# The last projection of a decoder trunk: weight sums by adding transfers, and a plain tile between two formed products

## The chip, the cores and the metric

The kernel runs on one core of one Trainium2 chip. The core has TensorE (PE, matrix products into PSUM), VectorE (DVE), ScalarE (ACT), GpSimd (POOL) and SyncE (SP, which issues most transfers between HBM and SBUF). Each engine works off its own queue in order, and engines wait for each other by semaphores. The metric is the device time of one execution in microseconds; the time given for a kernel is the median of its runs.

## The reference

One residual layer on 512 positions of width 1024, in float32:

```python
u = rmsnorm(x, ln1_g)
proj = u @ w_in                       # split into q, k, v, pool, z, xbc, dt, gates
y_a = dilated_attention(q, k, v) @ w_a
y_b = pool_mixer(pool_in) @ w_b
y_c = ssd_mixer(z, xbc, dt) @ w_c
x = x + (gates[0]*y_a + gates[1]*y_b + gates[2]*y_c) @ w_o
h = causal_dwconv(rmsnorm(x, ln2_g) @ w_up)      # 512 x 5632
a, v = h[..., :2816], h[..., 2816:]
x = x + (silu(a) * v) @ w_down                   # 2816 x 1024
return rmsnorm(x, final_g)
```

The change concerns only the last two lines: the product with `w_down` (here "the last projection") and its surroundings.

## The kernel before

**Products in three parts.** TensorE gets each float32 operand as a high part (rounded to the type fp32r) and a low part (what is left). `mm3` (L228) runs high x high for all k, then high x low, then low x high, and sums them in PSUM. So every weight tile goes through the same steps: `fetch` (SP loads it, tile `raw`, two buffers), `cast` (ACT writes the high part `wh`, three buffers), `low` (DVE writes the low part `wl`, two buffers), then the products. A `Job` is one weight tile with its products. While job n runs on TensorE, `prepare` (L1605) issues the low part of job n+1, the cast of job n+2 and the load of job n+3; the cast is put off to the next `step()` inside the job, in two halves. A job may bring a `form` (what the cast takes as its source) and a `then` (called right after its low part is issued). The order of PE, ACT, DVE and POOL is the order in which the program issues; only SP's loads are placed by a scheduler.

**The up projection.** `up_jobs` has 22 jobs of 48 products each. They alternate between the two halves a and v, two column tiles at a time. `up_evac` (L1182) does the convolution on ACT (L1184) and DVE (L1187); in v's half POOL multiplies a and v (L1192), and the high and low parts of the result (`fh`, `fl`, L1199 and L1200) or sums of neighbours for the scheme below (`sums_of`) follow.

**The last projection.** Of the 22 tiles of 128 rows of `w_down`, the first 16 go as two groups of 8. Each group is a two by two block product in 7 products of quarters rather than 8 (Strassen's scheme in Winograd's form). Four of the seven weight operands are sums or differences of quarters. The jobs are called "one" to "seven"; each has 24 products (two position blocks x 12). Their jobs stand between the up jobs: `EARLY` places the first group after up jobs 8 to 14, `LATE` places four jobs of the second group after up jobs 18 to 21. The other six row tiles are plain: `blocks_of(0)` makes the left half of the columns in a job of 48 products and one of 24, `blocks_of(1)` the right half, with the norm and the output. `down` (L1300) gives the end of the kernel: "seven", first plain tile, "four", second plain tile, "three", right half.

**The weight sums.** `quarters(g)` gives the quarters q(two, h) in HBM. `load` puts q(0,1) and q(1,1) into two tiles W (tag `xs`). DVE forms each operand with `diff` (L339), a subtraction over 128x2048, in W or in a freshly loaded `raw`: after the low part of "one", and as the `form` of "six", "seven" and "four" (of the first group after "three"). That is four per group.

**Banks.** "one", "six", "seven" and "four" go on in the same two PSUM banks (X, names p1, p6, p7, p4; the profile prints them as `p`): each adds its product on what is there. After each of them `plus` (L1217) lets DVE add the bank to the sum X1, and the next may not write before that. "two", "five" and "three" share the banks Z.

**Norm.** When the left half of a position block is complete, `early` issues `norm_early`: a square sum on ACT (L438) and a product with the norm's weight on POOL (L462). `blocks_of(0)` asks for it for all four blocks.

The kernel is built with `dynamic_dma_scratch_size=1024`. Before the change no transfer is issued from POOL.

Of the kernel before, what the change touches and what calls it, by code (L numbers as in the profile page):

```python
# [13 lines left out]
OP = mybir.AluOpType  # L14
# [69 lines left out]
def trunk(ctx: ExitStack, tc, out, x, rel_bias, ln1_g, w_in, b_gate, w_a, pool_w, pool_scale, w_b,  # L84
# [235 lines left out]
    def sums_of(f0, f1, ah, al, found):  # L320
# [3 lines left out]
        dve.tensor_tensor(sa[:, LO], f0[:, HI], f1[:, HI], OP.add)  # L324
        dve.tensor_tensor(sa[:, HI], sa[:, LO], f0[:, LO], OP.subtract)
        dve.tensor_tensor(sb[:, LO], f0[:, LO], f0[:, HI], OP.subtract)
        dve.tensor_tensor(sb[:, HI], f1[:, LO], sa[:, HI], OP.subtract)
# [854 lines left out]
    def up_evac(m, ps):  # L1182
# [11 lines left out]
        def later():  # L1194
            yield
            k = m - KF
            if k >= KS or k % 2:
# [4 lines left out]
                if k < KS:  # L1202
                    yield
                    for _ in sums_of(HC[k - 1], a, T("sah", F32R), T("sal", F32R),
                                     lambda j, h, l: FS.__setitem__((j, k // 2), (h, l))):
                        yield
# [10 lines left out]
    def plus(tb, h, what):  # L1217
        dve.tensor_tensor(X1[tb, h], X1[tb, h], what, OP.add)
# [45 lines left out]
    def into(banks, name, adds, first=False, close=True):  # L1264
        def use(i, product):
# [3 lines left out]
            for tb, h in adds(i):  # L1269
                plus(tb, h, banks[i])  # L1270
        return use

    def sevens_down(g, keep=False):
# [4 lines left out]
        def load():  # L1278
            for h in range(2):
                W.append(ypool.tile([P, 4, S], F32, name="w3", tag="xs"))  # L1280
                sp.dma_start(W[h], q(h, 1))

        two = job(q(1, 0), side("A12"), into(Z, "p2", lambda i: [(i, 0)], True))
        one = job(q(0, 0), side("A11"), into(X, "p1", lambda i: [(i, 0)], True))
        one.then = lambda: diff(W[0], W[0], one.raw)
        five = job(None, side(1), into(Z, "p5", lambda i: [(2 + i, 1)], True), lambda: W[0])
        if keep:
            three = job(q(1, 1), side(4), into(Z, "p3", lambda i: [], close=False))
            six = job(None, side(2), into(X, "p6", lambda i: [(i, 1)]), lambda: diff(W[1], W[1], W[0]))
        else:  # L1290
            three = job(None, side(4), into(Z, "p3", lambda i: [(i, 1)]), lambda: W[1])
            three.then = lambda: diff(W[1], W[1], W[0])
            six = job(None, side(2), into(X, "p6", lambda i: [(i, 1)]), lambda: W[1])
        seven = job(q(0, 0), side(3), into(X, "p7", lambda i: [(2 + i, 1)]),
                    lambda: diff(seven.raw, W[1], seven.raw))
        four = job(q(1, 0), side("A22"), into(X, "p4", lambda i: [(2 + i, 0)]),
                   lambda: diff(four.raw, four.raw, W[1]))
        return load, dict(two=two, one=one, five=five, three=three, six=six, seven=seven, four=four), Z

    def down(rest, opened):  # L1300

        plain = blocks_of(0, {}, (), ())
        yield rest["seven"]
        yield next(plain)
        yield rest["four"]
        yield from plain
# [60 lines left out]
    def blocks_of(h, acc, opened, keep):  # L1367
        def evac(tb, ps):
            t = X1[tb, h]
            dve.tensor_tensor(t, t, ps, OP.add)  # L1370
            if h == 0:
                running.append(early(tb))
                return
# [291 lines left out]
```

## Time and profile before

| | before |
|---|---|
| median of 3 runs | 1039.03 us (1038.7 to 1039.3) |
| the profiled execution | 1038.0 us |
| its span, first to last instruction | 1036.2 us |
| mean granted TensorE clock | 0.998 |
| TensorE busy | 1024.7 us (99% of the span) |
| DVE, ACT, POOL busy | 676.2, 473.8, 149.6 us |
| moved by transfers | 120.76 MB |

The profile is of one execution; all its times count from the start of the span. A row of a timeline gives start, length, engine, line of the kernel, operation and `output<-input` with shapes, and in brackets how long the engine stood idle before it and what ended that. A row of a table of stretches gives for each engine its busy time and number of instructions, then the granted clock, the share of time that the 16 DMA engines were busy, and GB/s. In a row of groups `x2 | 4.6, 2288` means two instructions, 4.6 us together, 2288 ns each on average, and then the idle time before them. Matmuls overlap, so the length of one (about 0.39 us) is longer than its share of a row of them.

### The profile page before, as it was taken

How to read it: one execution, taken by the hardware profiler on the slowest of the kernel's cores; microseconds unless marked ns; L12 is line 12 of the kernel's file. 1: busy time of each engine (PE TensorE's matmuls, PEld its weight loads, DVE VectorE, ACT ScalarE, POOL GpSimd, SP SyncE). 2: the span in 40 equal slices, each digit the busy share in tenths (PEclk: the TensorE clock that was granted, in tenths of full speed). 3: DMA queues.
4: the chain of work that ended last, by engine and by line, in shares of the span. 5: the costliest groups of instructions: out<-in, count | busy, mean ns of one | idle time of the engine just before them, and what ended most of it. 6: DMA issues, size and time to landing. Idle time of an engine off the chain costs nothing.

```text
span 1036.2 us, 13090 instructions
## 1 busy us (share of the span) xinstructions
PE 1024.7 (99%) x5204; PEld 859.7 (83%) x5204; DVE 676.2 (65%) x907; ACT 473.8 (46%) x765; POOL 149.6 (14%) x125
## 2 busy tenths in 40 slices
PE   9999999999999999999999999999999999999997
PEld 9898878898888878888888888898888888888785
DVE  6553566684356658766768656766768677666855
ACT  6432544442564364557445324545444443443332
POOL 1770000000000004210152500001111001111110
PEclk9999999999999999999999999999999999999999
DMA  8344312126222344542244525543233224323232
GB/s 280 123 131 134 116 47 75 31 64 200 82 82 82 98 132 115 144 136 69 66 149 153 172 82 204 175 140 114 82 115 122 89 82 163 122 90 114 82 122 82
DMA packets 119069, 120.76 MB, mean 117 GB/s; under 512 B 5316, under 2 KB 101383, under 8 KB 119008
## 3 DMA queue, kind: packets, MB, share of 16 engines
q1 hardware_dynamic: 118415, 119.07, 36.4%
q8 instruction: 41, 0.67, 0.3%
q10 hardware_dynamic: 592, 0.86, 0.2%
q14 instruction: 21, 0.16, 0.1%
HBM read 116.12 MB, written 2.22 MB: 114 GB/s over the span
## 4 chain that ended last, share of the span: by engine, by line
PE 96%; DVE 1%; ACT 1%; DMA 1%; issue 0%; ACTq 0%; DVEq 0%
PE pa L234 35%; PE pu L234 22%; PE pb L234 11%; PE pqk L234 9%; PE p L234 8%; PE pa L1516 2%; PE ps L670 1%; PE pu L1324 1%; PE ppw L234 1%; PE pt L698 1%; PE po L711 1%; PE py L996 1%; DMA xin<-in_x_dram 1%; PE pyo L1003 1%; PE pst L982 0%; PE pxs L950 0%
## 5 line engine op out<-in xcount | busy, mean ns | idle before, releaser
L215 DVE TENSOR_TENSOR wl<-raw,wh 128x2048 fp32r<-128x2048 f32 (+3 forms) x95 | 218.8, 2305 | 50.2 <-ACT wh L195 40.6
L195 ACT CAST wh<-raw 128x1024 fp32r<-128x1024 f32 (+3 forms) x188 | 189.4, 1026 | 68.0 <-DVE raw L339 26.0
L1187 DVE SCALAR_TENSOR_TENSOR hc<-pu,fcol,hc 128x510 f32<-128x510 f32 x88 | 65.8, 747 | 58.9 <-ACT hc L1184 57.3
L234 PE MATMUL pa<-uh,wh 128*128 128x512 f32 x384 | 98.5, 398 | 0.0
L234 PE MATMUL pa<-ul,wh 128*128 128x512 f32 x384 | 94.9, 389 | 0.0
L234 PE MATMUL pa<-uh,wl 128*128 128x512 f32 x384 | 94.9, 389 | 0.0
L234 PEld LDWEIGHTS pa<-ul,wh 128*128 128x128 f32 x384 | 72.1, 188 | 15.2
L234 PEld LDWEIGHTS pa<-uh,wl 128*128 128x128 f32 x384 | 72.1, 188 | 15.0
L234 PE MATMUL pu<-uh,wl 128*128 128x512 f32 (+1 forms) x352 | 83.7, 380 | 0.0
L234 PE MATMUL pu<-uh,wh 128*128 128x512 f32 (+1 forms) x352 | 83.5, 379 | 0.0
L234 PE MATMUL pu<-ul,wh 128*128 128x512 f32 (+1 forms) x352 | 83.5, 379 | 0.0
L234 PEld LDWEIGHTS pa<-uh,wh 128*128 128x128 f32 x384 | 70.3, 188 | 14.7 <-issue 0.7
L234 PEld LDWEIGHTS pu<-uh,wl 128*128 128x128 f32 x352 | 64.1, 188 | 12.8 <-DVE wl L215 0.3
L234 PEld LDWEIGHTS pu<-ul,wh 128*128 128x128 f32 x352 | 64.2, 188 | 12.5
L234 PEld LDWEIGHTS pu<-uh,wh 128*128 128x128 f32 x352 | 64.1, 188 | 12.4
L1192 POOL TENSOR_TENSOR hc<-hc 128x512 f32<-128x512 f32 x22 | 30.5, 1388 | 278.9 <-DVE hc L1187 243.1
L1184 ACT ACTIVATE hc<-pu,fcol,fcol 128x512 f32<-128x512 f32 x40 | 31.2, 780 | 81.3 <-PE pu L234 81.0
L958 POOL TENSOR_TENSOR xd<-xc,dec 128x512 f32<-128x512 f32 x6 | 6.4, 1060 | 334.1 <-DVE xc L952 315.2
L1085 ACT ACTIVATE sg<-pa,col 128x512 f32<-128x512 f32 x24 | 16.5, 688 | 55.3 <-PE pa L234 48.6
L691 ACT ACTIVATE sb<-sb,both 128x128 f32<-128x128 f32 (+1 forms) x72 | 30.1, 419 | 23.5 <-DVE both L688 13.4
L234 PE MATMUL pqk<-uh,wh 128*128 128x512 f32 x144 | 36.9, 394 | 0.0
L234 PE MATMUL pqk<-ul,wh 128*128 128x512 f32 x144 | 36.3, 390 | 0.0
(352 smaller groups left out, 1793.2 us busy)
## 6 DMA issues: line engine op xcount, KB each, us to landing
raw<-in_w_in_dram SPq DMA_DIRECT2D x25, 1024.0 KB
raw<-in_ffn_w_up_dram SPq DMA_DIRECT2D x22, 1024.0 KB
raw<-in_ffn_w_down_dram SPq DMA_DIRECT2D x11, 1024.0 KB
raw<-in_w_in_dram SPq DMA_DIRECT2D x20, 512.0 KB
raw<-in_w_o_dram SPq DMA_DIRECT2D x8, 1024.0 KB
raw<-in_w_b_dram SPq DMA_DIRECT2D x4, 1024.0 KB
al<-ad SPq DMA_DIRECT2D x16, 256.0 KB
w<-in_ffn_w_down_dram SPq DMA_DIRECT2D x4, 1024.0 KB
```

The source lines that it names most:

```text
L195: act.copy(job.high[:, :, o], job.raw[:, :, o])
L215: (eng or dve).tensor_tensor(l[:, :, o], job.raw[:, :, o], h[:, :, o].bitcast(F32), OP.subtract)
L234: pe.matmul(ps, l, r, start=first and n == 0, stop=last and n == total - 1, skip_group_check=again)
L670: pe.matmul(pss[i][:, o:o + w * P], q[r, n * P:(n + 1) * P], k[r, kb * P:(kb + w) * P], start=True, stop=True)
L691: act.activation(sb[:, off:off + w * P], sb[:, off:off + w * P], AF.Exp, bias=nm[:, n, h:h + 1], accum_out=ls[:, n, h:h + 1])
L698: pe.transpose(pt[:, o:o + P], sb[:, o:o + P], eye)
L711: pe.matmul(po[DH * hh:DH * hh + DH, n * P:(n + 1) * P], V[g, kb + i][:, (2 * cc + hh) * DH:(2 * cc + hh + 1) * DH], probs[2 * cc + hh, mb ...
L1085: act.activation(s, ps, AF.Sigmoid, bias=col[:, o:o + 1])
L1184: act.activation(t, ps, AF.Identity, bias=ff["c1"][:, ff["b"] + m:ff["b"] + m + 1], scale=fw(2, m))
L1187: dve.scalar_tensor_tensor(t[:, sh:], ps[:, :S - sh], fw(k, m), t[:, sh:], OP.mult, OP.add)
L1192: pool.tensor_tensor(a, a, t, OP.mult)
L1516: pe.matmul(first[2 * n + j][:, lo:hi], a[:, k, j * P:(j + 1) * P], b[:, k, lo:hi], start=a is wh and b is uh and k == 0, stop=a is wl and ...
```

## The change

- The quarters are combined by adding only. `load` brings q(0,0) and q(0,1) into the two tiles W. After the low part of "one" is issued, POOL issues transfers from HBM that add q(0,1) to W[0] and q(1,1) to W[1]; after "five" they add q(1,1) to W[0], after "six" q(1,0) to W[0]. Each 1 MB is cut into two transfers of 512 KB. That is 8 transfers per group. The eight `diff` calls of the two groups go, and "one", "five", "six", "seven" and "four" take W as it is.
- The signs that this moves go to the other side: `sums_of` gets a sign for two of its four operations, and `plus` subtracts for "six" and "seven".
- "one" now comes before "two" in both groups, "three" always loads its quarter, and the second group's `load` is called two up jobs earlier.
- `down` is now: first plain tile, "seven", second plain tile, "four", "three", right half. `early` for position blocks 2 and 3 is issued after "four" instead of after the second plain tile.

```diff
--- before.py
+++ after.py
@@ -317,14 +317,14 @@
 
     LO, HI = slice(0, 256), slice(256, S)
 
-    def sums_of(f0, f1, ah, al, found):
+    def sums_of(f0, f1, ah, al, found, s=1):
 
 
         sa, sb = T("sa"), T("sb")
-        dve.tensor_tensor(sa[:, LO], f0[:, HI], f1[:, HI], OP.add)
+        dve.tensor_tensor(sa[:, LO], f0[:, HI], f1[:, HI], OP.add if s > 0 else OP.subtract)
         dve.tensor_tensor(sa[:, HI], sa[:, LO], f0[:, LO], OP.subtract)
         dve.tensor_tensor(sb[:, LO], f0[:, LO], f0[:, HI], OP.subtract)
-        dve.tensor_tensor(sb[:, HI], f1[:, LO], sa[:, HI], OP.subtract)
+        dve.tensor_tensor(sb[:, HI], f1[:, LO], sa[:, HI], OP.subtract if s > 0 else OP.add)
         yield
         bh, bl = T("sbh", F32R), T("sbl", F32R)
         act.copy(ah, sa)
@@ -1202,7 +1202,7 @@
                 if k < KS:
                     yield
                     for _ in sums_of(HC[k - 1], a, T("sah", F32R), T("sal", F32R),
-                                     lambda j, h, l: FS.__setitem__((j, k // 2), (h, l))):
+                                     lambda j, h, l: FS.__setitem__((j, k // 2), (h, l)), -1):
                         yield
                 return
             t = T("f0", F32R)
@@ -1214,8 +1214,8 @@
 
     FS = {}
 
-    def plus(tb, h, what):
-        dve.tensor_tensor(X1[tb, h], X1[tb, h], what, OP.add)
+    def plus(tb, h, what, op=OP.add):
+        dve.tensor_tensor(X1[tb, h], X1[tb, h], what, op)
 
     def first_half(p, i):
         return [t[:, i * P:(i + 1) * P] for t in FS[0, p]]
@@ -1261,13 +1261,15 @@
             return lambda p, i: second_half(p, i + 2 * (j == "A22"))
         return lambda p, i: sums(j, p, i)
 
-    def into(banks, name, adds, first=False, close=True):
+    def into(banks, name, adds, first=False, close=True, final=False):
         def use(i, product):
             if first:
                 banks[i] = SM(name)
             product(banks[i], first, close, not first)
-            for tb, h in adds(i):
-                plus(tb, h, banks[i])
+            for tb, h, *op in adds(i):
+                plus(tb, h, banks[i], *op)
+            if final:
+                running.append(early(2 + i))
         return use
 
     def sevens_down(g, keep=False):
@@ -1278,32 +1280,34 @@
         def load():
             for h in range(2):
                 W.append(ypool.tile([P, 4, S], F32, name="w3", tag="xs"))
-                sp.dma_start(W[h], q(h, 1))
+                sp.dma_start(W[h], q(0, h))
+
+        def adding(at, *what):
+            def then():
+                for w, part in zip(at, what):
+                    for k in (0, 2):
+                        pool.dma_start(W[w][:, k:k + 2, :], part[:, k:k + 2, :], accum_op=OP.add)
+            return then
 
         two = job(q(1, 0), side("A12"), into(Z, "p2", lambda i: [(i, 0)], True))
-        one = job(q(0, 0), side("A11"), into(X, "p1", lambda i: [(i, 0)], True))
-        one.then = lambda: diff(W[0], W[0], one.raw)
+        one = job(None, side("A11"), into(X, "p1", lambda i: [(i, 0)], True), lambda: W[0])
+        one.then = adding((0, 1), q(0, 1), q(1, 1))
         five = job(None, side(1), into(Z, "p5", lambda i: [(2 + i, 1)], True), lambda: W[0])
-        if keep:
-            three = job(q(1, 1), side(4), into(Z, "p3", lambda i: [], close=False))
-            six = job(None, side(2), into(X, "p6", lambda i: [(i, 1)]), lambda: diff(W[1], W[1], W[0]))
-        else:
-            three = job(None, side(4), into(Z, "p3", lambda i: [(i, 1)]), lambda: W[1])
-            three.then = lambda: diff(W[1], W[1], W[0])
-            six = job(None, side(2), into(X, "p6", lambda i: [(i, 1)]), lambda: W[1])
-        seven = job(q(0, 0), side(3), into(X, "p7", lambda i: [(2 + i, 1)]),
-                    lambda: diff(seven.raw, W[1], seven.raw))
-        four = job(q(1, 0), side("A22"), into(X, "p4", lambda i: [(2 + i, 0)]),
-                   lambda: diff(four.raw, four.raw, W[1]))
+        five.then = adding((0,), q(1, 1))
+        three = job(q(1, 1), side(4), into(Z, "p3", lambda i: [] if keep else [(i, 1)], close=not keep))
+        six = job(None, side(2), into(X, "p6", lambda i: [(i, 1, OP.subtract)]), lambda: W[0])
+        six.then = adding((0,), q(1, 0))
+        seven = job(None, side(3), into(X, "p7", lambda i: [(2 + i, 1, OP.subtract)]), lambda: W[1])
+        four = job(None, side("A22"), into(X, "p4", lambda i: [(2 + i, 0)], final=keep), lambda: W[0])
         return load, dict(two=two, one=one, five=five, three=three, six=six, seven=seven, four=four), Z
 
     def down(rest, opened):
 
         plain = blocks_of(0, {}, (), ())
+        yield next(plain)
         yield rest["seven"]
-        yield next(plain)
+        yield from plain
         yield rest["four"]
-        yield from plain
         yield rest["three"]
         yield from blocks_of(1, opened, (0, 1), ())
 
@@ -1369,7 +1373,8 @@
             t = X1[tb, h]
             dve.tensor_tensor(t, t, ps, OP.add)
             if h == 0:
-                running.append(early(tb))
+                if tb < 2:
+                    running.append(early(tb))
                 return
             v0, xg0 = fin[tb]
             for _ in norm_late(t, fin["g"], v0, lambda xg1: ((xg1, xg1), (xg0, xg0)),
@@ -1432,13 +1437,13 @@
         first, between, _ = sevens_down(0)
         second_, last_, opened = sevens_down(1, keep=True)
         extra = {EARLY + i: between[w] for i, w in enumerate(
-            ("two", "one", "five", "three", "six", "seven", "four"))}
-        extra.update({LATE + i: last_[w] for i, w in enumerate(("two", "one", "five", "six"))})
+            ("one", "two", "five", "three", "six", "seven", "four"))}
+        extra.update({LATE + i: last_[w] for i, w in enumerate(("one", "two", "five", "six"))})
         for i, job in enumerate(up_jobs()):
             yield job
             if i == EARLY - 3:
                 yield Call(first)
-            if i == LATE - 1:
+            if i == LATE - 3:
                 yield Call(second_)
             if i in extra:
                 yield extra[i]
```

## The prediction

> **What bounds the kernel now.** I read the head of the page first, then the stretches of the last projection one by one, then the order of time around the one hole that they show.
>
> ```profile
> span 1036.2 us, 13090 instructions
> PE 1024.7 (99%) x5204; PEld 859.7 (83%) x5204; DVE 676.2 (65%) x907; ACT 473.8 (46%) x765; POOL 149.6 (14%) x125
> PE 96%; DVE 1%; ACT 1%; DMA 1%; issue 0%; ACTq 0%; DVEq 0%
> ```
>
> TensorE is busy for 1024.7 of 1036.2 us and carries 96% of the chain that ended last. The change leaves the number of products as it is, so it can win only what lies in TensorE's holes, in the part of the span that it touches. The next fence is the table by stretches, from the first undisturbed product of the up projection to the end.
>
> ```profile
> core 0: us, PE busy (x) PEld busy (x) DVE busy (x) ACT busy (x) POOL busy (x), PEclk, DMA share, GB/s
> 689.12:972.90 283.78, 283.78 (x1298) 236.70 (x1297) 202.06 (x213) 123.66 (x163) 27.51 (x20) 1.00 0.32 105
> 923.90:945.70 21.80, 21.80 (x98) 18.06 (x97) 16.05 (x14) 10.59 (x14) 2.90 (x2) 1.00 0.35 117
> 945.70:962.00 16.30, 16.30 (x73) 13.49 (x73) 9.19 (x10) 5.00 (x7) 0.00 (x0) 1.00 0.20 65
> 972.90:980.04 7.14, 5.42 (x25) 4.17 (x24) 6.48 (x7) 4.86 (x6) 3.02 (x2) 1.00 0.00 0
> 980.04:1029.30 49.26, 49.24 (x216) 40.43 (x216) 30.28 (x45) 14.82 (x28) 7.10 (x4) 1.00 0.31 108
> 1029.30:1036.20 6.90, 0.00 (x0) 0.00 (x0) 2.72 (x8) 1.65 (x4) 0.00 (x0) 0.72 0.39 150
> ```
>
> From 689.12 to 972.90 TensorE has no hole, though VectorE makes seven of the eight sums there and is 71% busy. The only holes are 7.14 - 5.42 = 1.72 us before 980.04, and the 6.90 us after the last product. The granted clock is 1.00 up to the last product, so no clock is to be won.
>
> Now the hole itself, in order of time: "six" of the second group ends, "seven" (tiles p and sbh) starts.
>
> ```profile
> 973.31 1.30 POOL L1192 TENSOR_TENSOR hc<-hc 128x512 f32<-128x512 f32 x1 [28.92 <-DVE hc L1187]
> 974.65 0.62 ACT L1199 CAST fh<-hc 128x512 fp32r<-128x512 f32 x1
> 975.30 0.69 DVE L1200 TENSOR_TENSOR fl<-hc,fh 128x512 fp32r<-128x512 f32 x1
> 975.44 1.71 POOL L1192 TENSOR_TENSOR hc<-hc 128x512 f32<-128x512 f32 x1 [0.82 <-ACT fh L1199]
> 975.91 3.38 DVE L215 TENSOR_TENSOR wl<-raw,wh 128x2048 fp32r<-128x2048 f32 x1
> 979.22 0.67 DVE L1218 TENSOR_TENSOR x<-x,p 128x512 f32<-128x512 f32 x1
> 980.04 1.17 PE L234 MATMUL p<-wh,sbh 128*128 128x512 f32 x4 [1.72 <-DVE x L1218]
> ```
>
> "Seven" goes on in the banks that "six" filled, so it may not start before VectorE has added them to X1 (L1218). That add stands on VectorE behind the low part of the next weight tile, which runs until 979.29; TensorE waits 1.72 us.
>
> **The change part by part.** *The eight sums go from VectorE.*
>
> ```profile
> L339 DVE TENSOR_TENSOR w<-w,w 128x2048 f32<-128x2048 f32 x2 | 4.6, 2288 | 0.0
> L339 DVE TENSOR_TENSOR raw<-raw,w 128x2048 f32<-128x2048 f32 x2 | 4.6, 2287 | 1.2 <-DMA raw<-in_ffn_w_down_dram 1.2
> L339 DVE TENSOR_TENSOR raw<-w,raw 128x2048 f32<-128x2048 f32 x2 | 4.6, 2284 | 0.0
> L339 DVE TENSOR_TENSOR w<-w,raw 128x2048 f32<-128x2048 f32 x2 | 4.6, 2282 | 0.0
> ```
>
> 8 x 2.29 = 18.3 us of VectorE. Products hide all of it but the hole, so by itself it is worth 0. The changed signs (add for subtract) leave each instruction at its size: 0.
>
> *A plain tile between "six" and "seven", and another between "seven" and "four".* While the first plain tile runs, the two adds of "six" get done. Lengths, from the chain of waits:
>
> ```profile
> 945.68 10.88 PE pu L234 x48
> 956.56 5.44 PE p L234 x24
> 962.00 10.89 PE pu L234 x48
> ```
>
> One product takes 10.88/48 = 0.227 us. "Six" ends at 972.89 + 5.44 = 978.33, and the plain tile (48 products, 10.88 us) holds until 989.21; the adds of "six" end by about 981. "Seven" then finds its banks free, and likewise "four" behind 5.44 us of the second plain tile. Gain: 1.72 us. What is late next is the low part of that plain tile. It takes the place of the 3.38 us row above, which ends at 979.29; the plain tile needs it from its ninth product, at 978.33 + 8 x 0.227 = 980.14. The margin is 0.85 us.
>
> *Sixteen adding transfers of 512 KB on POOL's queue.* Before, POOL issued no transfer, so their price has to be bounded. SP's own loads, issue and the consumer that waited for landing:
>
> ```profile
> 997.99 0.37 SPq L183 DMA_DIRECT2D raw<-in_ffn_w_down_dram  x1
> 1003.05 2.00 ACT L195 CAST wh<-raw 128x1024 fp32r<-128x1024 f32 x2 [4.64 <-DMA raw<-in_ffn_w_down_dram]
> 1005.04 0.37 SPq L183 DMA_DIRECT2D raw<-in_ffn_w_down_dram  x1
> 1008.76 0.62 ACT L195 CAST wh<-raw 128x512 fp32r<-128x512 f32 x1 [1.78 <-DMA raw<-in_ffn_w_down_dram]
> ```
>
> 1 MB (128x2048) lands in 5.06 us, 512 KB in 3.72. An adding transfer of 512 KB also has to read its 512 KB of destination, so I put its flight near the 1 MB load. Let p be the time from the issue of one to the point where POOL can issue the next. Ends: 0.37 us (POOL only issues, as SP does) and 10 us (twice the 1 MB load; the trace has no upper end). I take p = 5.5, the 1 MB row plus one issue of 0.37, on the cautious assumption that POOL is held until the one before has landed, since the kernel reserves only 1024 bytes of scratch for these transfers and cuts each into two. The Trainium skill's page "Collectives: The Full Stack" (Part 3: Why 7x under link rate) says an add on the DMA engines costs no cycles of its own but reads two sources and so halves the rate; no run here shows it yet.
>
> Where p matters: the second group's "five" to "seven", which stand closest.
>
> ```profile
> 918.25 2.28 DVE L215 TENSOR_TENSOR wl<-raw,wh 128x2048 fp32r<-128x2048 f32 x1
> 937.58 1.28 POOL L1192 TENSOR_TENSOR hc<-hc 128x512 f32<-128x512 f32 x1 [20.40 <-DVE hc L1187]
> 941.90 0.62 ACT L1199 CAST fh<-hc 128x512 fp32r<-128x512 f32 x1
> 948.26 2.28 DVE L215 TENSOR_TENSOR wl<-w,wh 128x2048 fp32r<-128x2048 f32 x1
> 959.58 1.03 ACT L195 CAST wh<-raw 128x1024 fp32r<-128x1024 f32 x1
> 962.86 2.28 DVE L339 TENSOR_TENSOR w<-w,w 128x2048 f32<-128x2048 f32 x1
> 965.06 1.27 DVE L1218 TENSOR_TENSOR x<-x,p 128x512 f32<-128x512 f32 x2
> 965.17 2.00 ACT L195 CAST wh<-w 128x1024 fp32r<-128x1024 f32 x2 [4.56 <-DVE w L339]
> 967.20 2.29 DVE L215 TENSOR_TENSOR wl<-w,wh 128x2048 fp32r<-128x2048 f32 x1 [0.87 <-ACT wh L195]
> ```
>
> - After "one": four transfers from 918.25 + 2.28 = 920.53. Behind them on POOL stands the product of gate and value (937.58), and ACT takes its result at 941.90. So 920.53 + 3p + 0.37 + 1.28 may reach 941.90: p up to 6.6.
> - After "five": its low part ends at 950.54, two transfers are in at 950.54 + 2p. The cast of "six" on ACT follows the cast that ends at 960.61; up to p = 5.0 nothing moves. It can run 4.6 us earlier than before (the sum at 962.86 is gone), and a larger p eats into that. The low part of "six" ends at 962.86 + 1.27 (adds of "five") + 2.29 = 966.4, or at 950.54 + 2p + 2.00 + 2.29 where that is later.
> - After "six": cast 2.00, low part 2.29, then two transfers. POOL must issue both before the gate product of the last up tile (973.31 before), and that one's fl (L1200) stands on VectorE directly ahead of the plain tile's low part. Sum for a large p: 950.54 + 2p + 4.29 (low part of "six") + p + 0.37 (both issued) + 1.30 + 0.65 + 0.61 (gate product, fh, fl, by the starts above) + 3.38 = 961.14 + 3p. It has to be in by 980.14: p up to 6.3.
>
> At p = 5.5 the low part of "six" ends at 966.4, and the plain tile's at 966.4 + 5.5 + 0.37 + 5.94 = 978.2 or, if VectorE is held up elsewhere, at 979.29 as before; 980.14 is kept: 0. The first group has an up tile between all its products and more room at each step. The casts of "seven" and "four" need transfers that are issued a tile or more earlier: 0.
>
> *Traffic.* Plain tiles aside, the quarters read for the two groups go from 13 MB (13 loads on SP) to 16 MB (8 loads on SP and 8 MB of adding transfers). The DMA engines are 35% busy in 923.90 to 945.70, 20% in the next stretch; another 2 MB of adds there fits, and loads that land some us later are covered by the double buffers: 0, at a price that is in p.
>
> *Norms of blocks 2 and 3 after "four".*
>
> ```profile
> 1005.69 7.10 POOL L462 TENSOR_TENSOR xg<-x,grow 128x512 f32<-128x512 f32 x4 [28.54 <-DVE x L1370]
> 1020.72 1.00 DVE L485 TENSOR_SCALAR xg<-xg,r,rt 128x512 f32<-128x512 f32 x2
> ```
>
> "Four" now ends about 1005.5, so half of POOL's 7.10 us starts where all four started before; the first use is at 1020.72 less 1.72: 0. The tail after the last product has the same instructions: 0.
>
> Sum: -1.72 us. The profiled execution would have a span of 1034.5 us and last 1036.3 instead of 1038.0; its own time is 1.03 us under the median of the runs, and with the same distance the median becomes 1039.03 - 1.72 = 1037.3 us (-0.17%).
>
> **The rivals.**
> *A. POOL is held longer than I take (slower).* Place: the last group, as above. From p = 6.3 on each us costs 3 us at the plain tile, and from 6.6 on another 3 through the four transfers after "one". At p = 7.1 the loss is 2.4 + 1.5 - 1.72 = 2.2 us, from where it counts as slower; at 7.5 it is 3.6 + 2.7 - 1.72 = 4.6, which gives 1043.6 us. For it: both margins are about 1 us, and SP's loads share the engines. Against it: a whole 1 MB lands in 5.06 us.
> *B. The hole only moves.* With p between 6.3 and 7.1 the plain tile waits for its low part about as long as "seven" waited for the add: at p = 6.8 it is 1.5 + 0.6 - 1.72 = 0.4, 1039.4 us. So the change would not do what its plain tile is for.
> *C. VectorE holds POOL's issue.* The rows above show the two engines holding each other: L215 takes 3.38 instead of 2.29 us, and L1192 1.71 instead of 1.30, where they overlap. If each issue waits out one low part, 2.29 us more for each, p becomes 7.8 and the last issue 2.66. The limits fall by 2.29/3 to 5.5 and 5.8: 3 x 2.3 + 3 x 2.0 - 1.72 = 11 us, so 1050 us. The Trainium skill ("SBUF — State Buffer", Who interferes with whom) states that transfers issued by GpSimd can be starved by VectorE; it names copies, casts and tensor_scalar in a two-port mode, and for two-input instructions only the read side. On the latter the trace agrees. Against C: between 945 and 975 VectorE runs two-input instructions only.
>
> **How the numbers follow.** Forecast (p up to 6.3): 0.52. B: 0.11. A: 0.27. C: 0.05. Another cause, as a late load: 0.05. 0.2% is 2.08 us, about what a measurement of this kernel can tell from no change. The forecast is only 0.36 us from it and the runs shown differ by 0.6 us, so a third of its chance, 0.18, counts as faster; the rest and B, with 0.02 of the unnamed, make 0.47 the same; A, C and the remainder 0.35 slower. Range: below, the forecast with 1 us for the runs' spread and a shorter tail, 1036.3; above, A up to p = 7.8 (4.5 + 3.6 - 1.72 = 6.4, with 1 us of spread), 1046.5. The likeliest case alone: 1036.6 to 1038.0.
>
> **What would show it.** TensorE without a hole from 689 to the last product near 1027.6, and "seven" starting straight behind the plain tile: right. L339 in the last projection gone, VectorE near 658 us. Four rows of transfers after "one" on POOL: their spacing is p. The gate product at or before 975 says A is off; if it stands at 977 or later, with the plain tile waiting for wl, A or B is on. ACT's casts of "six" waiting for a transfer past 963 would show p over 6. Wrong would also be a wait of an up tile for its load, or a hole in the first group.

## The result and the profile after

| | before | after |
|---|---|---|
| median, 11 runs each | 1038.69 us (1038.13 to 1041.57) | 1041.08 us (1038.17 to 1042.08) |
| ratio | 1 | 1.0019, 95% interval 1.0011 to 1.0027 |
| the profiled execution | 1038.0 us | 1040.81 us |
| its span | 1036.2 us | 1039.0 us |

The change makes the kernel slower by 2.4 us between the medians (0.19% by the ratio over the runs), where 1.7 us less were forecast. The head of the page of after, and its chain of waits by engine:

```profile
span 1039.0 us, 13113 instructions
PE 1026.9 (99%) x5204; PEld 861.9 (83%) x5204; DVE 656.6 (63%) x899; ACT 474.1 (46%) x765; POOL 168.9 (16%) x141
PE 91%; issue 3%; DVE 2%; ACT 1%; POOL 1%; DMA 1%; POOLq 0%; ACTq 0%; DVEq 0%
```

VectorE is relieved of 19.6 us, and POOL has 19.3 us more for 16 instructions more. TensorE's products are the same 5204, but it is busy 2.2 us longer, and the chain now leaves TensorE for some stretches ("issue", POOL, DMA). The table by stretches of after, with the columns of the prediction's table, shows where:

```profile
689.61:972.90 283.29, 283.29 (x1297) 236.44 (x1296) 186.53 (x205) 123.78 (x163) 45.82 (x35) 1.00 0.44 118
980.50:982.86 2.36, 0.01 (x1) 0.01 (x1) 2.36 (x3) 2.36 (x4) 0.00 (x0) 1.00 0.47 85
982.86:986.28 3.42, 3.42 (x8) 2.74 (x9) 3.42 (x4) 0.05 (x1) 0.00 (x0) 0.50 0.65 209
986.28:989.69 3.41, 3.41 (x16) 2.82 (x16) 0.52 (x1) 0.00 (x0) 0.00 (x0) 1.00 0.25 98
```

Up to 972.90 there is no hole, as before. The hole of 1.72 us ahead of "seven" is gone. In its place there is one of 2.36 us inside the plain tile, and behind it something new: a granted clock of 0.50 for 3.42 us. The chain of waits of after, in order of time, tells how the hole comes about (start, length, what):

```profile
953.72 1.21 POOL w L1289
954.93 4.71 issue
...
959.66 5.70 DMA w<-in_ffn_w_down_dram
...
965.43 2.00 ACT wh L195 x2
...
967.46 2.31 DVE wl L215
...
970.17 1.20 POOL w L1289
971.38 4.87 issue
...
977.03 1.78 POOL hc L1192
...
978.83 0.63 ACT fh L1199
...
980.52 2.29 DVE wl L215
...
982.86 10.94 PE pb L234 x40
```

POOL issues a transfer at 953.72 and can issue the next only at 959.66. That one lands after 5.70 us, "six" is cast (965.43) and gets its low part, POOL issues at 970.17 and again only after 4.87 us of "issue". Only then comes the last gate product (977.03), then fh, fl, and the plain tile's low part, which ends at 982.81. TensorE needed it at 980.50.

The two new terms: the hole, 2.36, and the slow products behind it. The 40 products from 982.86 take 10.94 us instead of 40 x 0.2267 = 9.07, so 1.87. With the 1.72 won that is +2.51 us; the first undisturbed product of the up projection started 0.49 us later (689.61 against 689.12), ahead of anything that is discussed here. Together 3.0, against 2.8 us between the spans.

POOL's rows between "one" of the second group and the hole; the two transfers after "five" stand in the chain above:

```profile
921.46 1.20 POOL L1289 DMA_DIRECT2D w<-in_ffn_w_down_dram  x1 [4.00 <-DVE hc L1187]
927.45 1.22 POOL L1289 DMA_DIRECT2D w<-in_ffn_w_down_dram  x1 [4.79 <-issue]
933.99 1.21 POOL L1289 DMA_DIRECT2D w<-in_ffn_w_down_dram  x1 [5.32 <-issue]
942.76 1.22 POOL L1289 DMA_DIRECT2D w<-in_ffn_w_down_dram  x1 [7.57 <-DVE hc L1187]
943.53 3.02 POOL L1192 TENSOR_TENSOR hc<-hc 128x512 f32<-128x512 f32 x2
...
970.17 1.20 POOL L1289 DMA_DIRECT2D w<-in_ffn_w_down_dram  x1 [9.30 <-DVE wl L215]
976.26 1.21 POOL L1289 DMA_DIRECT2D w<-in_ffn_w_down_dram  x1 [4.89 <-DVE hc L1187]
```

The spacing of two transfers behind one another is the prediction's p: 5.99, 6.54 and 8.77, then 5.94 (from 953.72 to 959.66 in the chain above) and 6.09. The time from issue to landing of all 16, and the stretches of the first three spacings:

```profile
DMA to landing us min/median/max: 5.6/5.8/8.5
```

```profile
921.46:927.45 5.99, 5.99 (x29) 4.94 (x28) 2.93 (x5) 3.44 (x6) 1.20 (x1) 1.00 0.56 89
927.45:933.99 6.54, 6.54 (x30) 5.43 (x29) 5.61 (x4) 2.80 (x3) 1.22 (x2) 1.00 0.73 161
933.99:942.76 8.77, 8.77 (x40) 7.27 (x39) 2.93 (x5) 3.56 (x4) 1.20 (x1) 1.00 0.90 240
```

SP's loads beside them:

```profile
930.70 3.77 SPq L183 DMA_DIRECT2D raw<-in_ffn_w_up_dram  x2
```

p is the flight plus about 0.3 us, and it is largest where the engines are busiest (DMA share 0.90, 240 GB/s): SP issued two loads of 1 MB from 930.70 to 934.5. That these loads make the 8.77 us is read from the shares and not shown: no run took them away, and in the first group, where two such loads are issued at 783.72 to 788.7, the spacings are 6.23, 6.02 and 6.59 us at shares of 0.52, 0.69 and 1.01. So the size of this one is not fully explained, but it came back in each kernel with 1024 bytes (8.95, 9.07 and 9.37 us).

### The profile page after: what moved, and what is told of

It is laid out like the page before. It is cut to its first block, busy times and chain, and to the rows that moved or that the text cites. A ratio compares the mean times of both kernels' runs of the same rounds, so it can differ in the third digit from the quotient of the medians.

```text
span 1039.0 us, 13113 instructions
## 1 busy us (share of the span) xinstructions
PE 1026.9 (99%) x5204; PEld 861.9 (83%) x5204; DVE 656.6 (63%) x899; ACT 474.1 (46%) x765; POOL 168.9 (16%) x141
## 4 chain that ended last, share of the span: by engine, by line
PE 91%; issue 3%; DVE 2%; ACT 1%; POOL 1%; DMA 1%; POOLq 0%; ACTq 0%; DVEq 0%
PE pa L234 35%; PE pu L234 18%; PE pb L234 11%; PE pqk L234 9%; PE p L234 6%; PE pa L1521 2%; PE ps L670 1%; PE pu L1328 1%; PE ppw L234 1%; PE pt L698 1%; PE po L711 1%; DVE wl L215 1%; PE py L996 1%; PE pa L1478 1%; POOL w L1289 1%
## 5 line engine op out<-in xcount | busy, mean ns | idle before, releaser
L215 DVE TENSOR_TENSOR wl<-raw,wh 128x2048 fp32r<-128x2048 f32 (+3 forms) x90 | 204.1, 2270 | 49.0 <-ACT wh L195 36.7
L195 ACT CAST wh<-raw 128x1024 fp32r<-128x1024 f32 (+3 forms) x178 | 179.0, 1025 | 33.5 <-DMA raw<-in_w_in_dram 14.0
L234 PE MATMUL pa<-uh,wh 128*128 128x512 f32 x384 | 98.5, 398 | 0.0
L234 PE MATMUL pa<-ul,wh 128*128 128x512 f32 x384 | 94.9, 389 | 0.0
L234 PE MATMUL pa<-uh,wl 128*128 128x512 f32 x384 | 94.9, 389 | 0.0
L234 PEld LDWEIGHTS pa<-ul,wh 128*128 128x128 f32 x384 | 72.1, 188 | 15.2
L234 PEld LDWEIGHTS pa<-uh,wl 128*128 128x128 f32 x384 | 72.1, 188 | 14.9
L234 PE MATMUL pu<-uh,wl 128*128 128x512 f32 (+1 forms) x352 | 83.6, 380 | 0.0
L234 PE MATMUL pu<-uh,wh 128*128 128x512 f32 (+1 forms) x352 | 83.6, 379 | 0.0
L234 PE MATMUL pu<-ul,wh 128*128 128x512 f32 (+1 forms) x352 | 83.5, 379 | 0.0
L234 PEld LDWEIGHTS pa<-uh,wh 128*128 128x128 f32 x384 | 70.3, 188 | 14.7 <-issue 0.7
L234 PEld LDWEIGHTS pu<-uh,wl 128*128 128x128 f32 x352 | 64.1, 188 | 12.6 <-DVE wl L215 0.2
L234 PEld LDWEIGHTS pu<-ul,wh 128*128 128x128 f32 x352 | 64.2, 188 | 12.5
L234 PEld LDWEIGHTS pu<-uh,wh 128*128 128x128 f32 x352 | 64.1, 188 | 12.4
L234 PE MATMUL pqk<-uh,wh 128*128 128x512 f32 x144 | 36.9, 394 | 0.0
L234 PE MATMUL pqk<-ul,wh 128*128 128x512 f32 x144 | 36.3, 390 | 0.0
```

What stands on the lines that cost most here:

```text
L195: act.copy(job.high[:, :, o], job.raw[:, :, o])
L215: (eng or dve).tensor_tensor(l[:, :, o], job.raw[:, :, o], h[:, :, o].bitcast(F32), OP.subtract)
L234: pe.matmul(ps, l, r, start=first and n == 0, stop=last and n == total - 1, skip_group_check=again)
```

## The experiments

Theory H: POOL is held because the descriptor scratch of 1024 bytes has room for one adding transfer, so that each waits until the one before has landed. Rivals: L, the transfers are slow since loads share the engines with them, with room in the scratch or without; V, VectorE holds POOL's issue (the prediction's rival C).

| kernel | median, us | ratio to before, 95% interval |
|---|---|---|
| after with 2304 bytes of scratch | 1036.09 | 0.998 (0.9971 to 0.9988) |
| the reorder alone | 1036.39 | 0.9981 (0.9972 to 0.999) |
| after, last two gate products on VectorE | 1036.95 | 0.9988 (0.9979 to 0.9997) |
| the adding transfers alone | 1044.88 | 1.0066 (1.0053 to 1.008) |
| after, gate products of the tile before on VectorE | 1036.67 | 0.9987 (0.9977 to 0.9997) |
| 2304 bytes, transfers of 1 MB | 1035.97 | 0.9978 (0.9968 to 0.9987) |
| after with 1152 bytes of scratch | 1036.54 | 0.9982 (0.9973 to 0.9992) |
| the reorder, low part later by 3 operations | 1037.87 | 0.9998 (0.9988 to 1.0008) |
| the same, 4 operations | 1038.22 | 1.0 (0.9991 to 1.001) |
| the same, 5 operations | 1040.06 | 1.0019 (1.0009 to 1.0028) |
| the same, 6 operations | 1041.51 | 1.0034 (1.0021 to 1.0047) |

Before ran beside them at 1038.17 to 1038.44 us.

**More scratch.**

```diff
-    nc = _bacc.Bacc("TRN2", ..., dynamic_dma_scratch_size=1024)
+    nc = _bacc.Bacc("TRN2", ..., dynamic_dma_scratch_size=2304)
```

> The changed kernel with 2304 instead of 1024 bytes of scratch for the transfers that POOL issues; nothing else differs. Theory H (POOL is held because the scratch has room for one adding transfer at a time): the spacing of the issues within a group falls from about 6.0 us to the 1.2 us of an issue, the gate products of the last up tile stand at 970 to 975 us instead of 977, the hole of 2.36 us before the ninth product of the first plain tile goes, and with it the slow stretch behind it; span 1034.5 to 1035.0, ratio to the kernel before about 0.9985 (1037.0 us). Theory L (the transfers land late because SP's loads share the engines): spacing falls but the cast of "six" still waits until about 965 or later and a hole of 1 us or more stays; 1039 us or more. Theory V (VectorE holds POOL's issue): the spacing stays at 5 us or more; no change against the changed kernel, 1041 us.

POOL's rows of this kernel, and one stretch from the up projection to just before the last product:

```profile
920.74 4.91 POOL L1289 DMA_DIRECT2D w<-in_ffn_w_down_dram  x4 [4.01 <-DVE hc L1187]
936.89 1.28 POOL L1192 TENSOR_TENSOR hc<-hc 128x512 f32<-128x512 f32 x1 [11.24 <-DVE hc L1187]
...
950.50 2.45 POOL L1289 DMA_DIRECT2D w<-in_ffn_w_down_dram  x2 [6.56 <-DVE wl L215]
966.30 2.43 POOL L1289 DMA_DIRECT2D w<-in_ffn_w_down_dram  x2 [13.35 <-DVE wl L215]
969.56 1.28 POOL L1192 TENSOR_TENSOR hc<-hc 128x512 f32<-128x512 f32 x1 [0.83 <-DVE hc L1187]
```

```profile
689.70:1026.80 337.10, 337.10 (x1530) 280.72 (x1528) 220.29 (x254) 143.29 (x197) 57.21 (x42) 1.00 0.41 113
```

The four issues take POOL 4.91 us together, 1.2 each, the first gate product of each tile comes 6.6 and 7.5 us earlier than in after (936.89 and 969.56 against 943.53 and 977.03), and TensorE has no hole in 337.10 us. The flights themselves are longer (median 7.9 us instead of 5.8, largest 12.8), as L says of a shared engine, but nobody waits for them. H holds. V falls, since VectorE works in the same way and POOL is not held; L falls, since the cast of "six" starts at 960.06 and no hole is left.

**1152 bytes, an eighth more than 1024.** The same line with 1152.

> The changed kernel with its descriptor scratch at 1152 bytes instead of 1024, an eighth more. Theory H says that POOL is held while the scratch has no room for one more transfer. If an eighth more is room for a second one (1024 being just too little), the issues go in pairs: the second of a pair about 1.2 us behind the first, the third and fourth of job one only when the first and second have landed, so that the four are issued within some 8 to 9 us instead of 21 to 22; no hole before the plain tile, 1036.2, between 1035.7 and 1036.9. If it is not, everything stays as in the changed kernel: spacing 6.0 to 6.6 us, a hole of about 2.4 us and 1038 to 1042. A rival to H (a longer scratch helps in another way, by so much a byte) gives spacings a little under 6 us and a hole a little shorter.

POOL's rows behind "one" of the second group:

```profile
921.53 2.45 POOL L1289 DMA_DIRECT2D w<-in_ffn_w_down_dram  x2 [4.00 <-DVE wl L215]
927.83 1.22 POOL L1289 DMA_DIRECT2D w<-in_ffn_w_down_dram  x1 [3.84 <-issue]
930.37 1.21 POOL L1289 DMA_DIRECT2D w<-in_ffn_w_down_dram  x1 [1.32 <-issue]
```

Two go at once, the third waits out the flight of the first (6.3 us from 921.53), the fourth that of the second. So it is room for a number of transfers, one at 1024 bytes and two at 1152, and no gain by the byte; two suffice for a time that cannot be told from that with 2304 bytes.

**The reorder alone**: before, with the plain tiles moved and the norms of blocks 2 and 3 after "four", and `diff` as before.

```diff
         plain = blocks_of(0, {}, (), ())
+        yield next(plain)
         yield rest["seven"]
-        yield next(plain)
+        yield from plain
         yield rest["four"]
-        yield from plain
         yield rest["three"]
...                                    # and `early` of blocks 2 and 3 after "four", as in the change
```

> The kernel before with the new order at the end alone (a plain tile before "seven" and before "four", norms of blocks 2 and 3 after "four"); the sums stay on VectorE and no transfer is issued from POOL. Theory H: the hole of 1.72 us goes and no other comes, span 1034.5, ratio 0.9983 to 0.9985 (about 1037.0 us): the reorder was worth what the prediction said, and the adding transfers took it back. Rival (the plain tile has a hole of its own, because its low part is late with or without transfers): a hole of 1 to 2.5 us before the ninth product of the plain tile, 1038.5 us or more.

Its stretch:

```profile
689.70:1026.80 337.10, 337.10 (x1532) 280.80 (x1532) 238.50 (x262) 143.01 (x197) 35.52 (x26) 1.00 0.31 104
```

TensorE is without a hole here too, with VectorE's eight sums still in place (238.50 instead of 220.29 us). 1036.39 is 1.92 us under before as run beside it (1038.31); 1.72 were forecast for this part. And within the intervals it is no slower than after with 2304 bytes (1036.09), which has the transfers too: the relief of VectorE by 18 us is worth nothing that can be measured.

**The adding transfers alone**: after with the job order and the norms of before.

```diff
         plain = blocks_of(0, {}, (), ())
-        yield next(plain)
         yield rest["seven"]
-        yield from plain
+        yield next(plain)
         yield rest["four"]
+        yield from plain
...                                    # and `early` as before
```

> The changed kernel with the old order at its end ("seven" straight behind "six", the norms as before): the adding transfers alone. Theory H: the gate product of the last up tile is late as in the changed kernel (977), VectorE reaches the adds of "six" only at about 982.7, and "seven" starts at 983.3 instead of 978.8: a hole of 4.5 us in place of 1.72, with the granted clock at half for some us behind it; 1043 to 1044 us (ratio 1.004). Without a held POOL: the hole is 1.7 us or less, 1037 to 1038.7 us.

The row behind TensorE's hole, and two stretches, the first of which begins inside the hole:

```profile
983.53 2.05 PE L234 MATMUL p<-wh,sbh 128*128 128x512 f32 x4 [5.31 <-DVE x L1218]
```

```profile
981.60:985.01 3.41, 1.48 (x4) 1.22 (x5) 3.41 (x5) 2.27 (x3) 0.00 (x0) 0.50 0.02 2
985.01:988.42 3.41, 3.41 (x10) 2.65 (x9) 1.78 (x1) 0.00 (x0) 0.00 (x0) 0.50 0.12 21
```

Before's hole of 1.72 us ahead of "seven" has become one of 5.31, and the clock is at 0.50 from 981.60 to 988.42, of which 4.9 us lie behind the hole ("seven" takes 8.02 instead of 5.44 us). That is 3.6 + 2.6 = 6.2 us, against 6.57 between the medians; a hole of 4.5 us and 1043 to 1044 us were expected, so both came out larger. The gate product comes at 977.05, as late as in after (977.03). So the reorder does not cause the loss; it makes it smaller.

**Where the lateness begins.** Two kernels take gate products off POOL's queue, with the scratch left at 1024: those of the last up tile, or those of the tile before it.

```diff
-        pool.tensor_tensor(a, a, t, OP.mult)
+        (dve if m >= KF + 20 else pool).tensor_tensor(a, a, t, OP.mult)     # first kernel: the last tile
...
-        pool.tensor_tensor(a, a, t, OP.mult)
+        (dve if m - KF in (18, 19) else pool).tensor_tensor(a, a, t, OP.mult)     # second kernel: the tile before
```

> The changed kernel with the two gate products of the last up tile (the ones behind the transfers of "six" on POOL) on VectorE instead of POOL. Theory H: the spacing of the transfers stays at 6 us, but nothing on the way to the plain tile's low part stands behind them any more; VectorE has 2 x 0.7 us more; the hole of 2.36 us goes or falls under 0.5 us, about 1037.2 us (ratio 0.9985). Theory L or V (the low part is late for another reason): the hole stays at 2 us or more, 1040 to 1041 us.

> The changed kernel, its scratch left at 1024 bytes; only the two gate products of the last up tile but one (the ones at 943.53 in the changed kernel, behind the four transfers of job one) go to VectorE. Theory H (each adding transfer holds POOL until the one before has landed, 6.0 to 6.6 us, once 8.8), with the place settled: the whole lateness of 2.36 us before the plain tile begins with these two products. They were due some 2.8 us before 943.53 and the chain from them (fh, fl, low part of the next up tile, low part of five, its transfers, cast of six, its transfers, the last two gate products) hands the lateness on. Without it low part of five is back at about 950.5, the last product on POOL at about 974.5 to 976.3, the hole before the plain tile under 0.3 us, and the time about that of the reorder alone: 1036.4, between 1035.9 and 1037.2. Rival (the last limit binds by itself: three transfers of 6 to 6.6 us behind one another do not fit between the low part of five and the last products, wherever five stands): the hole stays at 1 to 2.4 us and the time is 1038 to 1041.

In the first, the transfers are spaced as in after (6.2, 6.1 and 9.4 us behind "one"), the products of the tile before still come at 943.85, and the plain tile's low part is nevertheless ready at 977.19 + 2.29 = 979.48: the last product waits for no transfer, and this profile has no hole. Its runs spread from 1035.89 to 1039.99 us, and the longest has a mean granted clock of 0.996, the others 0.998 or 0.999, so a hole is likely left in some of them. In the second, POOL and VectorE show:

```profile
942.30 1.22 POOL L1289 DMA_DIRECT2D w<-in_ffn_w_down_dram  x1 [7.87 <-issue]
950.35 1.21 POOL L1289 DMA_DIRECT2D w<-in_ffn_w_down_dram  x1 [6.83 <-DVE wl L215]
956.58 1.22 POOL L1289 DMA_DIRECT2D w<-in_ffn_w_down_dram  x1 [5.03 <-DMA w<-in_ffn_w_down_dram]
967.30 1.21 POOL L1289 DMA_DIRECT2D w<-in_ffn_w_down_dram  x1 [9.51 <-DVE wl L215]
973.29 1.22 POOL L1289 DMA_DIRECT2D w<-in_ffn_w_down_dram  x1 [4.78 <-issue]
```

```profile
977.56 2.28 DVE L215 TENSOR_TENSOR wl<-raw,wh 128x2048 fp32r<-128x2048 f32 x1
```

The fourth transfer still goes at 942.30, but nothing stands behind it, the transfers of "five" go at 950.35 instead of 953.72, and the plain tile's low part ends at 979.84, in time: no hole. So the three transfers of the last group do fit at a spacing of 6.0 to 6.2 us. What made after late came in at the products behind the four transfers of "one", and the rest of the chain, with no slack left, handed it on. Either place alone would have been harmless: it takes both.

**Transfers of 1 MB**, with 2304 bytes: a candidate for a faster kernel, since it has half the issues.

```diff
-                    for k in (0, 2):
-                        pool.dma_start(W[w][:, k:k + 2, :], part[:, k:k + 2, :], accum_op=OP.add)
+                    pool.dma_start(W[w][:, 0:4, :], part[:, 0:4, :], accum_op=OP.add)
```

> The changed kernel with 2304 bytes of descriptor scratch, and each pair of 512 KB adding transfers as one of 1024 KB: eight issues on POOL instead of sixteen. If the price of an issue goes with its descriptors, one takes about 2.4 us and nothing changes: 1036.1, between 1035.6 and 1036.7. If the scratch has no room for the second transfer while the first is under way, POOL is held again between the two of job one for a whole 1 MB flight (about 10 us, an estimate from 5.6 to 5.8 us per 512 KB), the last two gate products still come in time because the later transfers stand alone, and the time is 1036 to 1037; a hole before the plain tile and 1038 or more would say that they do not.

Its row for "one", and the time to landing of all eight:

```profile
921.00 2.63 POOL L1288 DMA_DIRECT2D w<-in_ffn_w_down_dram  x2 [4.01 <-DVE hc L1187]
```

```profile
DMA to landing us min/median/max: 8.5/8.9/14.4
```

An issue of 1 MB takes 1.3 us of POOL, not 2.4: the price goes by the instruction far more than by the size. One MB lands in 8.5 us at the least where half of it takes 5.6. At 1035.97 us it is the fastest kernel of the study and beats both before and after, but it cannot be told from the other kernels without a hole.

**The clock behind a hole.** That the clock falls was in none of the prediction's cases. Four kernels take the reorder alone, which has no hole, and make the first plain tile's low part later by computing its first quarter n times more (to the same values).

```diff
+        for _ in range(job.again):     # 3, 4, 5 or 6 for the first plain tile, else 0
+            dve.tensor_tensor(l[:, 0:1, :], job.raw[:, 0:1, :], h[:, 0:1, :].bitcast(F32), OP.subtract)
...                                    # and the reorder, as above
```

> The reorder alone (no adding transfers, 1036.39 us), with the first quarter of the first plain tile's low part computed three times more ahead of it on VectorE, to the same values: only that low part is later, by three operations on 128x512 of 0.57 to 0.85 us (a quarter of 2.29 or of 3.38 us). In the reorder alone it ends at 979.79, and TensorE's first product with it starts at 980.59: 0.8 us of slack. So the hole is 0.9 to 1.8 us. Theory G (the clock falls behind a hole once it is longer than something between the 1.72 us of before and the 2.36 us of after): full clock behind it, time 1036.4 plus the hole, 1037.3 to 1038.2. Theory N (it is not the hole's length but something in the changed kernel's stage): the same here.

> The same with four such operations: the low part 2.3 to 3.4 us later, a hole of 1.5 to 2.6 us. Theory G: if the hole is over about 2.3 us the granted clock falls to 0.5 for some 3.5 us behind it and the time is 1036.4 plus the hole plus 1.8, 1040 to 1041; if it is under 1.8, 1038 to 1038.3. Theory N: 1036.4 plus the hole alone, 1037.9 to 1039.0, and full clock behind it at any length.

> Five extra operations ahead of the plain tile's low part. With four the hole was 2.00 us at full clock, and three of the four took 0.69 us: the hole is about 2.7 us, longer than the 2.36 us of the changed kernel, behind which the clock fell to 0.5. Theory G (length of the hole, with the edge between 2.0 and 2.36 us): a granted clock of 0.5 for about 3.5 us behind it, and a time of 1038.2 + 0.7 + 1.8 = 1040.7, between 1040.2 and 1041.3. Theory N (not the length alone): full clock and 1038.9, between 1038.4 and 1039.4. A spread of the runs over 1.5 us would say that the clock falls in some runs only.

> Six extra operations: a hole of about 3.4 us. Theory G: a granted clock of 0.5 for about 3.5 us behind it, 1041.4, between 1040.9 and 1042. Theory N: full clock, 1039.6, between 1039.1 and 1040.1.

TensorE's row behind the hole, of 3, 4, 5 and 6 operations (L237 is the product line, L234 before):

```profile
982.19 1.21 PE L237 MATMUL pb<-wl,fh 128*128 128x512 f32 x4 [1.27 <-DVE wl L218]
```

```profile
982.17 1.20 PE L237 MATMUL pb<-wl,fh 128*128 128x512 f32 x4 [2.00 <-DVE wl L218]
```

```profile
982.80 1.20 PE L237 MATMUL pb<-wl,fh 128*128 128x512 f32 x4 [2.73 <-DVE wl L218]
```

```profile
983.67 1.55 PE L237 MATMUL pb<-wl,fh 128*128 128x512 f32 x4 [3.46 <-DVE wl L218]
```

The runs of each kernel, in us:

| hole in the profile | runs | the runs |
|---|---|---|
| 1.27 | 10 | 1037.27 to 1038.62 |
| 2.00 | 10 | 1038.01 to 1039.08 |
| 2.36 (after) | 11 | 1038.17, 1039.59, 1039.92; eight from 1040.81 to 1042.08 |
| 2.73 | 10 | five from 1038.98 to 1039.46; five from 1040.65 to 1042.16 |
| 3.46 | 5 | 1041.43 to 1043.16 |

Holes of 1.27 and 2.00 us cost about their length (1.5 and 1.8 us over the reorder alone). At 2.73 us the runs fall into two groups, and the profiled one, at full clock, belongs to the shorter; the gap between the groups is 1.2 us and between their middles (1039.12 and 1040.76) 1.6 us, about the 1.87 that the slow clock cost in after. At 3.46 all five runs are long and the profile shows the clock at 0.50. So neither theory as put holds: there is no edge in length between 2.00 and 2.36, and a growing share of the runs loses the clock.

The mean granted clock that is on record for each run bears this out. It is 0.998 or 0.999 in all runs of the reorder with 3 and 4 operations. With 5 it is 0.998 in the five shorter runs and 0.995 to 0.997 in the five longer; with 6 it is 0.995 to 0.997 in all. Of after it is 0.998 in the three shortest runs and 0.996 or 0.997 in seven of the eight from 1040.81 on; the eighth (1041.34 us) has 0.999, and its length is not explained. One stretch of 3.42 us at half clock makes 0.0016 of the span.

The traces also show what it depends on. In each of the 13 traces all changes of the granted clock that are recorded lie whole multiples of 3.413 us apart: in after it is 1.00 from 6.65, 0.50 from 982.86 (286 times 3.413 later), 1.00 from 986.28 and 0.50 from 1034.06, behind the last product. So each trace has a grid of windows of 3.41 us. The first recorded edge lies between 4.7 and 6.7 us in the seven traces with a hole near 980, so it does not come at the same place in each run. The windows around the hole with 5 operations, then with 6:

```profile
977.72:981.13 3.41, 2.35 (x11) 1.62 (x9) 3.27 (x5) 0.00 (x0) 0.00 (x0) 1.00 0.00 0
981.13:984.54 3.41, 1.74 (x8) 1.43 (x9) 3.41 (x2) 0.00 (x0) 0.00 (x0) 1.00 0.13 26
984.54:987.96 3.42, 3.42 (x17) 2.83 (x16) 2.33 (x5) 2.92 (x4) 0.00 (x0) 1.00 0.34 127
```

```profile
980.93:984.34 3.41, 0.67 (x3) 0.57 (x4) 3.38 (x3) 0.00 (x0) 0.00 (x0) 1.00 0.00 0
984.34:987.76 3.42, 3.42 (x10) 2.65 (x9) 2.33 (x3) 1.85 (x3) 0.00 (x0) 0.50 0.44 153
```

With 5 operations an edge cuts the hole into 1.06 and 1.67 us of idle time, and the clock stays. With 6, one window holds 2.74 us of it (3.41 - 0.67), and the next window is at half clock. In after one window, 979.45 to 982.86, holds the whole hole of 2.36. Taken over all windows of the 13 traces, the one that follows is at full clock up to 1.72 us of idle time in a window (the hole of before, which lies in a single window) and at half from 2.06 on (from 1.93, which is 3.41 - 1.48, with the adding transfers alone, where the window itself is at half already), without an exception. So it is not the length of the hole that decides, but how much of it falls into one window, and the same hole can cost the clock in one run and not in the next. Hole lengths may also vary from run to run. Of before, two of the first 11 runs (1040.95 and 1041.57) stand out in the same way, and none of the 77 that were run later; no clock is on record for these two, and what happened in them is open.

The Trainium skill's page "TensorE: Matmul & The Clock Gate" (Part 1: The HAM clock gate) has TensorE at half clock after at least one idle window of about 3.4 us, and says that the window runs freely. The grid of 3.41 us and the 0.50 agree with that. The window need not be idle from end to end here, since 2.36 of its 3.41 us were enough in after; so the page's rule of thumb (in the section Why this matters for your kernels), to avoid idle gaps over some 3 us, does not hold for this kernel.

## Why the prediction was wrong

- **The reorder, -1.72 us: right.** Alone it gave 1.92 us, and "seven" starts straight behind the plain tile.
- **The sums on VectorE worth nothing: right.** Reorder with and without them: 1036.39 and 1036.09 us, with overlapping intervals.
- **POOL held until the transfer before has landed, since the scratch is 1024 bytes: right, and shown** by 1152 and 2304 bytes. It was called cautious; it was simply the case.
- **p = 5.5: too small; this is the step that failed.** Measured 5.9 to 6.6, and 8.77 behind "one". The flight was put at a 1 MB load (5.06); it is 5.6 to 5.8 for 512 KB alone. The larger part is that p was one number for the whole stage: the third spacing after "one" is 8.77, most likely since that transfer flies beside two loads of the up projection, which no run shows.
- **"After one", p up to 6.6: about 0.4 too high, and the mean spacing of 7.1 (5.99 + 6.54 + 8.77 = 21.3) broke it.** fh started at 945.33 instead of 941.90, and the low part of "five" ended at 953.3 instead of 950.54, so 2.8 us late. Three small terms of the sum were put too low as well: POOL's first issue came at 921.46 instead of 920.53, the product started 0.77 us after the last issue instead of 0.37, and it took 1.78 instead of 1.28 us. With them the limit is about (21.3 - 2.8)/3 = 6.2, an estimate from these rows. The margin of about 1 us was given as small, but traffic was costed at "a price that is in p", from the mean DMA share of 0.35 over the stretch before. After, the share over the third spacing is 0.90.
- **"After six", p up to 6.3: right by itself, in part by luck.** The sum 961.14 + 3p gives 979.4 at p = 6.1; with "one" out of the way it measured 979.84, in time. The luck is that the low part took 2.28 us where the sum has 3.38, while its other terms were too small by more than that. With "five" 2.8 us late it comes to 982.2, measured 982.81.
- **Rivals.** What happened is between A and B: a hole of 2.36 instead of 1.72 us, so by holes alone +0.64 us, rival B's size, by A's place "after one". That A's price at p = 7.1, 2.2 us, lies near the measured 2.4 is luck: it takes 2.4 us of lateness from a limit "after six" that p = 6.1 did not pass, and has no term for the clock. The signs that were named for A or B came: the gate product at 977.03, the plain tile waiting for wl, the cast of "six" at 965.43. C did not occur: with more scratch issues took 1.2 us each beside the same work of VectorE.
- **"No clock is to be won": true, but one was to be lost.** 1.87 us of the loss are the slow products behind the hole (half of 3.42 us at clock 0.50 is 1.71 of them), a term that the sum and all rivals lacked. With it, B's 0.64 becomes 2.5 us. Before's hole of 1.72 us showed no such fall in its trace. The range held the result, on account of A.

## What to carry to other kernels

An engine that issues transfers from a scratch of its own can stand still when that scratch is full, as POOL did here: count how many fit, and look at what is queued behind them on that engine, before costing the flight; here 128 bytes more of scratch turned a loss of 2.4 us into a gain of 1.6. A limit for several transfers in a row must be checked with the longest spacing that is to be expected at that place, not with the mean of the stage (here loads that share the engines are the likeliest reason for it, not shown), and a lateness that two steps can each absorb alone is not absorbed when both have used their slack. A hole in a bounding TensorE can cost some 1.7 us more than its length once over about 2 us of it fall into one window of the clock's 3.41 us grid, so moving a hole is not free even when it stays about the same size.

## What was not expected of the hardware

- The granted clock changes on a grid of 3.41 us. It fell to 0.50 for one window with holes of 2.36 and 3.46 us and for two with 5.31, and stayed at 1.00 with 1.27, 2.00 and (in the profiled run) 2.73: what counts is the idle time in one window, with the edge between 1.72 and 2.06 us.
- POOL's issue of an adding transfer takes 1.2 us for 512 KB and 1.3 us for 1 MB, where SP's plain load takes 0.37.
- Several adding transfers in flight slow each other (median to landing 5.8 us with one, 7.1 with two, 7.9 with up to four in flight), yet the last of four is in sooner than when each waits for the one before: 14.4 us at most after the first issue (920.74 to 923.0 + 12.1) against 27 (921.46 to 942.76 + 5.7).
